# A hybrid decoder layer on one core: the group preparation, group end, substitution and output rows recorded behind the reading of a PSUM bank

## The chip, the cores and the metric

One core of one Trainium2 chip. The metric is the device time of one execution in microseconds (us); times of several executions are given as their median. The engines by the profile's names: PE multiplies matrices (PEld is its weight load), DVE, ACT and POOL work on vectors, SP issues nearly all DMAs. Every engine takes its instructions in the order in which the program recorded them.

## What is computed

One decoder layer over 2048 tokens of 1024 channels, all in float32:

```python
h = rms_norm(x, pre_norm_w)
p = h @ w_in                                  # r k v z + two low ranks | conv | pool | 3 gates
y_a = rwkv7_branch(token_shift(p_rwkv), ...)  # a state of 64 x 64 for each of 8 heads, token by token
y_b = short_conv_branch(p_conv, conv_w)
y_c = pool_branch(p_pool, pool_w, pool_scale)
merged = sum_n sigmoid(p_gate[n]) * (y[n] @ w_branch[n])
x = x + rms_norm(merged @ w_out, post_norm_w)
```

## The kernel before

**Products.** Tokens are handled in two halves of 1024. A *product* (`product`, L180) multiplies a piece of 512 x 128 weights with 512 tokens: 12 matmuls of 128x512, because operands and weights are each split into a high and a low part (`hi`, `lo`; tiles h.., l.., wh, wl) and three of the four combinations are made (L183, L184, L185). ACT makes the high part of the weights (L142), POOL the low one (L144). A `Pair` (L190) makes two tiles of 128 columns for two blocks of 512 tokens in seven products instead of eight: the products T1, T2, T3, T4 work on sums and differences (tiles hT, lT) and are added to others. They share three banks of PSUM, one called `ch` and two called `mm`. So a bank is read in the midst of its use: `act.copy(p1, ch)` after B11 and `act.copy(u2, ch)` after T2; `dve.tensor_tensor(p1, p1, b2)` after B21 (L253), `u2 += bb` after B22 (L257) and `p5 += ch` after T3 (L261). A product that adds to a bank, or begins anew in it, cannot start until that reading is done. T4 of a pair (`last`, through `flush`) is put off until the next pair has made B11 and T1; it adds to the `ch` that L261 reads.

**What runs beside the products.** Each `yield` in a job stands behind a product. There `execute` prepares weights (`supply`), issues stores that are due (`after_product`, which also takes one piece of work from the list `puts`) and advances the *sides* by one step each. I call what is recorded between two products an *interval*. The sides are the RWKV groups (`rwkv_groups`; 16 groups of 128 tokens, groups 0 to 7 in the first half, 8 to 15 in the second), the norm and operands of the second half (`stage_ops`), the mixing of the pooling branch (`mix_pooled`), loads and splits of later operands (`fill`), and sums for the last stage (`out_sums`).

**A group** (`rwkv_group`, L688) has a *main chain*: small matmuls into `rk` banks (16 times 64x128 and so on), their masked copies G on DVE, a store of G to DRAM and a load back as NB, a forward *substitution* of 15 rows on NB and Tt (L760 and L761, two DVE instructions a row, in four portions of 4, 4, 4 and 3 rows), a store of Tt to DRAM (`td`) and a load back as TT, a DVE transpose Td (L777), matmuls with Td (L785), X and TT (L792), a second DVE transpose T1 (L800), matmuls with it (L811), and then the state, chunk by chunk (R, U, state). Beside it run, one step per interval, the *preparation* of the next group (`group_head`: kk, S, ta, f, BK, XA, r) and the *end* of the last group (`group_tail`: d, q, m, y). In `step` (L692) these two are advanced first and then the interval is left, so in the recorded order they stand after the main chain's work and before whatever the job does when it resumes: the reading of the bank. The same holds for the substitution, which stands in the main chain itself.

**The output stage** is eight pairs (`out_pair`) of output rows. For each of the four tiles of a pair, `last` (L1092, L1093: scale by the norm, add x) is put on the list `puts` and taken in a later interval by `after_product`, so before that interval's bank is read.

What sets the order is this, at the head of each interval:

```python
for _ in j.run():          # a job, up to its next yield
    supply(1)
    after_product()        # stores, one of puts
    for side in sides:
        side.advance()     # main chain, then end of the last group, then preparation of the next
```

Of the kernel before, what the change touches and what calls it, by code (L numbers as in the profile page):

```python
# [53 lines left out]
def trunk_kernel(ctx, tc, x, pre_norm_w, post_norm_w, w_in, mu_shift, rwkv_w0, rwkv_w_up,  # L54
# [132 lines left out]
    sums = [pool]  # L187
    tail = [None]

    class Pair:  # L190
# [42 lines left out]
        def run(self):  # L233
# [5 lines left out]
            act.copy(p1[:, 16:], ch)  # L239
            bb = mm_bank()  # L240
# [3 lines left out]
            act.copy(p5[:, 16:], bb)  # L244
            yield from flush()
# [3 lines left out]
            act.copy(u2[:, 16:], ch)  # L249
            b2 = mm_bank()  # L250
            product(b2, take(), ops["B21"], True)
            yield
            dve.tensor_tensor(p1[:, 16:], p1[:, 16:], b2, ALU.add)  # L253
            sink(0, 0, p1[:, 16:], p1)
            product(bb, take(), ops["B22"], False)
            yield
            dve.tensor_tensor(u2[:, 16:], u2[:, 16:], bb, ALU.add)  # L257
            sink(0, 1, u2[:, 16:], u2)
            product(ch, take(), ops["T3"], False)
            yield  # L260
            dve.tensor_tensor(p5[:, 16:], p5[:, 16:], ch, ALU.add)  # L261
            sink(1, 1, p5[:, 16:], p5)

            def last():
                product(ch, take(), ops["T4"], False)
                yield
                sink(1, 0, ch, None)
# [27 lines left out]
    def single(ops, c, sink):  # L295

        def body():
# [6 lines left out]
            act.copy(p1[:, 16:], ba)  # L304
            product(bb, a1, h["T1"], True, False)
            yield
            product(ba, a2, h["B21"], False)
            yield
            first = sink(0, ba)
            product(bb, a2, h["B22"], False)  # L310
            yield
            dve.tensor_tensor(p1[:, 16:], p1[:, 16:], bb, ALU.add)
            second = sink(1, p1[:, 16:])
# [19 lines left out]
    def after_product():  # L333
        for dst, src in stores.pop(0):
            sp.dma_start(dst, src)
        stores.append([])
        if puts:
            puts.pop(0)()
# [192 lines left out]
    def rwkv_single(half, h, c):  # L531
# [8 lines left out]
        def sink(b, val):  # L540
# [6 lines left out]
            def products(upw):  # L547
                (uh, ul) = upw
                for n, bias in enumerate((hw0, ha0)):
                    ns = half_of(n)  # L550
                    for i in range(NCT):
# [7 lines left out]
                        if i == 1:  # L559
                            yield  # L560
                    yield
            return products
# [126 lines left out]
    def rwkv_group(g, head, before, following):  # L689
# [4 lines left out]
        def step(n=1, begin=False):  # L694
            if begin and following is not None:
                after[0] = group_head(following)
            for _ in range(n):
                next(before, None)
                if after[0] is not None:
                    try:  # L700
                        next(after[0])
                    except StopIteration as e:
                        after[0], got[0] = None, e.value
                yield

# [52 lines left out]
        for j in range(15):  # L758
            n = 15 - j
            dve.tensor_tensor(tmp[:, :, :n], bc(NBt[:, j, j + 1:], 1, 8), bc(Tt[:, :, j], 2, n), ALU.mult)  # L760
            dve.tensor_tensor(Tt[:, :, j + 1:], Tt[:, :, j + 1:], tmp[:, :, :n], ALU.add)  # L761
            if j in (3, 7, 11):
# [613 lines left out]
```

## Time and profile before

| | |
|---|---|
| three runs, us | 2309.71, 2313.94, 2318.79 (median 2313.94) |
| the profiled execution, us | 2305.26 |
| its span, first to last instruction, us | 2303.5 |
| PE busy | 2172.0 us, 94% |
| DVE busy | 1398.6 us, 61% |
| POOL busy | 1320.7 us, 57% |
| ACT busy | 896.0 us, 39% |
| mean granted clock of PE | 0.968 |

The span and the views belong to the profiled execution; 1.76 us of its time lie outside the span. It is 8.68 us under the median and 4.45 us under the fastest of the three runs. Roughly, groups 0 to 7 run from 200 to 1010 us, groups 8 to 15 from 1150 to 1900 us, the merge of the branches ends near 2130 us and the output pairs fill the rest. A wait of an engine is idle time in front of an instruction; the profile puts it down to the instruction whose semaphore came last.

### The profile page before, as it was taken

Reading aid. Unit: us, or ns where it says so; the run is one execution under the profiler, and the core shown is the slowest. Engines: PE = TensorE matmul, PEld = TensorE weight load, DVE = VectorE, ACT = ScalarE, POOL = GpSimd, SP = SyncE. Lnnn points to the kernel's source line nnn. Section 1 sums busy time; section 2 is a strip of 40 time slices with the busy share of each in tenths; the row PEclk is TensorE's granted clock in tenths of the full one; section 3 lists DMA queues with packets and bytes.
Section 4 is the critical chain, followed back from the end, with each engine's and each line's share of the span. In section 5 each row is a group of like instructions: output and inputs, shape, how many; then the busy total and the mean of one; then the engine's idle time right before and its main releaser. Section 6 shows DMA issues by size and latency. Waiting matters only on the chain.

```text
span 2303.5 us, 47215 instructions
## 1 busy us (share of the span) xinstructions
PE 2172.0 (94%) x18514; PEld 1752.8 (76%) x18514; DVE 1398.6 (61%) x2214; ACT 896.0 (39%) x1777; POOL 1320.7 (57%) x1105
## 2 busy tenths in 40 slices
PE   5999999999999999989989999899999999999898
PEld 4788777777787877768878787777878788787786
DVE  7413777777848646635476867756475663655754
ACT  5444433442434345444533423244343521313343
POOL 7657565665656555436765655455565445555554
PEclk7989999999999999989999999999999999999999
DMA  3243323243547427343522323355464855898974
GB/s 104 87 142 120 103 62 91 66 141 106 155 131 213 121 89 218 104 159 124 160 83 55 100 54 107 88 166 160 131 186 116 252 147 146 271 315 280 317 223 143
DMA packets 471800, 336.20 MB, mean 146 GB/s; under 512 B 107477, under 2 KB 389274, under 8 KB 471578
## 3 DMA queue, kind: packets, MB, share of 16 engines
q1 hardware_dynamic: 471578, 333.19, 47.8%
q8 instruction: 145, 2.38, 0.4%
q14 instruction: 77, 0.63, 0.1%
HBM read 220.76 MB, written 112.33 MB: 145 GB/s over the span
## 4 chain that ended last, share of the span: by engine, by line
PE 64%; DVE 15%; DMA 5%; issue 5%; ACT 3%; POOL 2%; SPq 1%; DVEq 0%; POOLq 0%; ACTq 0%
PE ch L183 10%; PE ch L185 9%; PE ch L184 9%; PE mm L183 8%; PE mm L184 7%; PE mm L185 7%; DVE Ttmp L760 3%; DVE Tt L761 3%; PE rk L599 2%; PE rk L717 2%; POOL wl L144 1%; PE rk L841 1%; PE rk L833 1%; PE rk L849 1%; DMA ly<-yD 1%
## 5 line engine op out<-in xcount | busy, mean ns | idle before, releaser
L144 POOL TENSOR_TENSOR wl<-ws,wh 128x512 fp32r<-128x512 f32 x492 | 681.9, 1390 | 572.4 <-ACT wh L142 534.8
L142 ACT CAST wh<-ws 128x512 fp32r<-128x512 f32 x492 | 304.1, 619 | 233.7 <-PE mm L184 81.2
L183 PE MATMUL ch<-hT,wh 128*128 128x512 f32 x864 | 357.1, 413 | 29.4 <-DVE p L261 22.3
L185 PE MATMUL ch<-hT,wl 128*128 128x512 f32 x864 | 344.2, 398 | 0.4 <-POOL wl L144 0.4
L184 PE MATMUL ch<-lT,wh 128*128 128x512 f32 x864 | 344.4, 399 | 0.0
L183 PE MATMUL mm<-hB,wh 128*128 128x512 f32 x600 | 241.6, 403 | 2.8 <-ACT p L304 2.8
L184 PE MATMUL mm<-lB,wh 128*128 128x512 f32 x600 | 234.3, 390 | 0.0
L185 PE MATMUL mm<-hB,wl 128*128 128x512 f32 x600 | 234.1, 390 | 0.0
L183 PEld LDWEIGHTS ch<-hT,wh 128*128 128x128 f32 x864 | 167.0, 193 | 73.0 <-issue 22.6
L144 POOL TENSOR_TENSOR wl<-s,wh 128x512 fp32r<-128x512 f32 x64 | 86.7, 1355 | 200.7 <-ACT wh L142 197.0
L185 PEld LDWEIGHTS ch<-hT,wl 128*128 128x128 f32 x864 | 166.6, 193 | 38.0 <-POOL wl L144 1.3
L184 PEld LDWEIGHTS ch<-lT,wh 128*128 128x128 f32 x864 | 167.0, 193 | 32.0
L213 POOL TENSOR_TENSOR ws<-ws,s 128x512 f32<-128x512 f32 x128 | 181.3, 1417 | 1.6 <-DMA ws<-in_w_in 1.6
L1025 POOL TENSOR_TENSOR g<-g 128x512 f32<-128x512 f32 x64 | 86.2, 1353 | 112.5 <-DVE g L1021 97.0
L183 PEld LDWEIGHTS mm<-hB,wh 128*128 128x128 f32 x600 | 112.5, 188 | 29.7 <-ACT p L304 3.6
L183 PE MATMUL mm<-hT,wh 128*128 128x512 f32 x296 | 122.8, 415 | 10.6 <-DVE p L253 7.0
L185 PEld LDWEIGHTS mm<-hB,wl 128*128 128x128 f32 x600 | 112.6, 188 | 24.4
L184 PEld LDWEIGHTS mm<-lB,wh 128*128 128x128 f32 x600 | 112.8, 188 | 21.5
L183 PE MATMUL ch<-hB,wh 128*128 128x512 f32 x288 | 119.7, 416 | 7.0 <-DVE g L1021 3.6
L185 PE MATMUL ch<-hB,wl 128*128 128x512 f32 x288 | 116.5, 404 | 10.4 <-POOL wl L144 10.4
L761 DVE TENSOR_TENSOR Tt<-Tt,Ttmp 128x120 f32<-128x120 f32 (+14 forms) x240 | 117.3, 489 | 8.3
L185 PE MATMUL mm<-hT,wl 128*128 128x512 f32 x296 | 118.7, 401 | 0.0
(281 smaller groups left out, 4625.7 us busy)
## 6 DMA issues: line engine op xcount, KB each, us to landing
ws<-in_w_in SPq DMA_DIRECT2D x260, 256.0 KB
g<-gD SPq DMA_DIRECT2D x96, 256.0 KB
gD<-p SPq DMA_DIRECT2D x48, 256.0 KB
ly<-yD SPq DMA_DIRECT2D x48, 256.0 KB
ws<-in_w_branch SPq DMA_DIRECT2D x48, 256.0 KB
mD<-g SPq DMA_DIRECT2D x32, 256.0 KB
ws<-oD SPq DMA_DIRECT2D x32, 256.0 KB
xr<-in_x SPq DMA_DIRECT2D x32, 256.0 KB
```

The lines of the kernel that those rows point to most:

```text
L142: act.copy(hi, src)
L144: pool.tensor_tensor(lo, src, hi.bitcast(F32), ALU.subtract)
L183: pe.matmul(bank, hi[:, k, :], th[k], start=start and k == 0, stop=False, skip_group_check=True)
L184: pe.matmul(bank, hi[:, k, :], tl[k], start=False, stop=False, skip_group_check=True)
L185: pe.matmul(bank, lo[:, k, :], th[k], start=False, stop=stop and k == HK - 1, skip_group_check=True)
L213: sums[0].tensor_tensor(w[o], w[a], w[b], op)
L599: both(lambda h, hs: pe.matmul(bank[hs, a * 64:a * 64 + 64], src[hs, a], ident[hs, hs], start=True, stop=True))
L717: both(lambda h, hs: pe.matmul(bgs[n][hs, i * P:(i + 1) * P], BK[hs, n, 2 * i + c], XA[hs, 2 * i + c].rearrange("p x t -> p (x t)"), start ...
L760: dve.tensor_tensor(tmp[:, :, :n], bc(NBt[:, j, j + 1:], 1, 8), bc(Tt[:, :, j], 2, n), ALU.mult)
L761: dve.tensor_tensor(Tt[:, :, j + 1:], Tt[:, :, j + 1:], tmp[:, :, :n], ALU.add)
L833: both(lambda h, hs: pe.matmul(r3[hs, i], G[hs, 1, 0, a], vt[hs, a], start=True, stop=False, skip_group_check=True))
L1025: pool.tensor_tensor(acc[b], acc[b], gs[b], ALU.add)
```

## The change

A second kind of yield, `yield READ`, marks the point behind the reading of a bank. A function given to `aside` is run there, and so is one piece of `puts`. The preparation, the end and the four portions of the substitution are given to `aside`; the rest of the main chain and the other sides stay where they were. For groups 8 to 14 the number of intervals between the load of TT and the transpose Td grows from two to three, as groups 0 to 7 have it.

```diff
+    READ = True
+    asides = []
+    def aside(f):
+        asides.append(f)
+    def run_asides():
+        while asides:
+            asides.pop(0)()
...
             product(b2, take(), ops["B21"], True)
             yield
             dve.tensor_tensor(p1[:, 16:], p1[:, 16:], b2, ALU.add)
+            yield READ
             sink(0, 0, p1[:, 16:], p1)
             product(bb, take(), ops["B22"], False)
             yield
             dve.tensor_tensor(u2[:, 16:], u2[:, 16:], bb, ALU.add)
+            yield READ
             sink(0, 1, u2[:, 16:], u2)
             product(ch, take(), ops["T3"], False)
             yield
             dve.tensor_tensor(p5[:, 16:], p5[:, 16:], ch, ALU.add)
+            yield READ
             sink(1, 1, p5[:, 16:], p5)
             def last():
                 product(ch, take(), ops["T4"], False)
                 yield
+                yield READ
                 sink(1, 0, ch, None)
...
         for dst, src in stores.pop(0):
             sp.dma_start(dst, src)
         stores.append([])
-        if puts:
-            puts.pop(0)()
...
             for _ in range(n):
-                next(before, None)
-                if after[0] is not None:
-                    try:
-                        next(after[0])
-                    except StopIteration as e:
-                        after[0], got[0] = None, e.value
+                aside(beside)
                 yield
+        def beside():
+            next(before, None)
+            if after[0] is not None:
+                try:
+                    next(after[0])
+                except StopIteration as e:
+                    after[0], got[0] = None, e.value
...
-        for j in range(15):
-            n = 15 - j
-            dve.tensor_tensor(tmp[:, :, :n], bc(NBt[:, j, j + 1:], 1, 8), bc(Tt[:, :, j], 2, n), ALU.mult)
-            dve.tensor_tensor(Tt[:, :, j + 1:], Tt[:, :, j + 1:], tmp[:, :, :n], ALU.add)
-            if j in (3, 7, 11):
-                yield from step()
-        yield from step(1, True)
+        def substitute(js):
+            for j in js:
+                n = 15 - j
+                dve.tensor_tensor(tmp[:, :, :n], bc(NBt[:, j, j + 1:], 1, 8), bc(Tt[:, :, j], 2, n), ALU.mult)
+                dve.tensor_tensor(Tt[:, :, j + 1:], Tt[:, :, j + 1:], tmp[:, :, :n], ALU.add)
+        for j in range(0, 15, 4):
+            aside(lambda: substitute(range(j, min(j + 4, 15))))
+            yield from step(1, j == 12)
...
-        yield from step(3 if g < 8 else 2)
+        yield from step(3 if g < 15 else 2)
...
-            for _ in j.run():
-                supply(1)
-                after_product()
-                for side in sides:
-                    side.advance()
+            for read in j.run():
+                if read:
+                    run_asides()
+                    if puts:
+                        puts.pop(0)()
+                else:
+                    supply(1)
+                    after_product()
+                    for side in sides:
+                        side.advance()
+            run_asides()
         if not first:
             for _ in flush():
-                after_product()
+                pass
             while puts or stores[0] or stores[1]:
+                if puts:
+                    puts.pop(0)()
                 after_product()
```

The other readings of a bank (the ACT copies of a `Pair`, `single`, the products of the low ranks, `merge_tile`) get a `yield READ` in the same way, and `Side.finish` runs the asides after each step. The first group of each half has its preparation before the chain begins, as steps of its own that are not given to `aside`.

Three places in the recorded order, all on DVE. The first is the substitution of group 4, in a gate pair: `u..` is u2 += bb (L257), `p..<-..ch` is p5 += ch (L261; L277 in the changed file), Ttmp and Tt are the rows of the substitution, d is the end of group 3. Before:

```order
L257 TENSOR_TENSOR u_6851<-u_6851,mm 128x512
L760 TENSOR_TENSOR Ttmp<-NB,Tt 128x8x7
L761 TENSOR_TENSOR Tt<-Tt,Ttmp 128x8x7
L760 TENSOR_TENSOR Ttmp<-NB,Tt 128x8x6
L761 TENSOR_TENSOR Tt<-Tt,Ttmp 128x8x6
L760 TENSOR_TENSOR Ttmp<-NB,Tt 128x8x5
L761 TENSOR_TENSOR Tt<-Tt,Ttmp 128x8x5
L760 TENSOR_TENSOR Ttmp<-NB,Tt 128x8x4
L761 TENSOR_TENSOR Tt<-Tt,Ttmp 128x8x4
L675 TENSOR_TENSOR d<-d,v 128x512
L261 TENSOR_TENSOR p_6785<-p_6785,ch 128x512
```

And with the change:

```order
L272 TENSOR_TENSOR u_6850<-u_6850,mm 128x512
L786 TENSOR_TENSOR Ttmp<-NB,Tt 128x8x11
L787 TENSOR_TENSOR Tt<-Tt,Ttmp 128x8x11
L786 TENSOR_TENSOR Ttmp<-NB,Tt 128x8x10
L787 TENSOR_TENSOR Tt<-Tt,Ttmp 128x8x10
L786 TENSOR_TENSOR Ttmp<-NB,Tt 128x8x9
L787 TENSOR_TENSOR Tt<-Tt,Ttmp 128x8x9
L786 TENSOR_TENSOR Ttmp<-NB,Tt 128x8x8
L787 TENSOR_TENSOR Tt<-Tt,Ttmp 128x8x8
L277 TENSOR_TENSOR p_6780<-p_6780,ch 128x512
L786 TENSOR_TENSOR Ttmp<-NB,Tt 128x8x7
L787 TENSOR_TENSOR Tt<-Tt,Ttmp 128x8x7
```

Each reading has moved ahead of one portion of the substitution (and of the d beside it); the portion before that still stands in front of it.

The second place is group 8, a conv pair, where the transpose Td follows kk of the next preparation. Before:

```order
L261 TENSOR_TENSOR p_12140<-p_12140,ch 128x512
L877 SCALAR_TENSOR_TENSOR silu<-silu,p_12140 128x512
L904 TENSOR_TENSOR u_11963<-u_11963,silu 128x512
L608 TENSOR_TENSOR kk<-k,vec 128x512
L777 STREAM_TRANSPOSE Td<-TT 128x512
L877 SCALAR_TENSOR_TENSOR silu<-silu,ch 128x512
L904 TENSOR_TENSOR p_11842<-p_11842,silu 128x512
L621 SCALAR_TENSOR_TENSOR S<-smask,sw 128x512
```

With the change:

```order
L277 TENSOR_TENSOR p_12140<-p_12140,ch 128x512
L904 SCALAR_TENSOR_TENSOR silu<-silu,p_12140 128x512
L931 TENSOR_TENSOR u_11963<-u_11963,silu 128x512
L630 TENSOR_TENSOR kk<-k,vec 128x512
L904 SCALAR_TENSOR_TENSOR silu<-silu,ch 128x512
L931 TENSOR_TENSOR p_11842<-p_11842,silu 128x512
L804 STREAM_TRANSPOSE Td<-TT 128x512
L643 SCALAR_TENSOR_TENSOR S<-smask,sw 128x512
```

Td now stands behind one more interval, that of the product T4 whose bank silu reads. Every later group of this half begins one interval later than the one before it did, seven in all at the end.

The third place is the second output pair: so, post and xr belong to the output rows (L1092, L1093; L1120, L1121 in the changed file), lm to the sums for later pairs. Before:

```order
L257 TENSOR_TENSOR u_22292<-u_22292,mm 128x512
L1092 SCALAR_TENSOR_TENSOR p_22208<-p_22208,so,post 128x512
L1093 TENSOR_TENSOR xr<-xr,p_22208 128x512
L1058 TENSOR_TENSOR lm<-lm 128x256
L1059 TENSOR_TENSOR lm<-lm 128x256
L1060 TENSOR_TENSOR lm<-lm 128x2x128
L1061 TENSOR_TENSOR lm<-lm 128x2x128
L261 TENSOR_TENSOR p_22234<-p_22234,ch 128x512
```

With the change:

```order
L272 TENSOR_TENSOR u_22290<-u_22290,mm 128x512
L1086 TENSOR_TENSOR lm<-lm 128x256
L1087 TENSOR_TENSOR lm<-lm 128x256
L1088 TENSOR_TENSOR lm<-lm 128x2x128
L1089 TENSOR_TENSOR lm<-lm 128x2x128
L277 TENSOR_TENSOR p_22234<-p_22234,ch 128x512
L1120 SCALAR_TENSOR_TENSOR p_22206<-p_22206,so,post 128x512
L1121 TENSOR_TENSOR xr<-xr,p_22206 128x512
```

The output row's two instructions have moved behind the reading of `ch`.

## Rows read from the trace of the kernel before

**Rows 1.** The page: busy time of PE and DVE, and the chain by engine.
```profile
PE 2172.0 (94%) x18514; PEld 1752.8 (76%) x18514; DVE 1398.6 (61%) x2214; ACT 896.0 (39%) x1777; POOL 1320.7 (57%) x1105
...
PE 64%; DVE 15%; DMA 5%; issue 5%; ACT 3%; POOL 2%; SPq 1%; DVEq 0%; POOLq 0%; ACTq 0%
```
**Rows 2.** Timeline of PE, first matmuls of two products: start, length, instruction, [idle before <-releaser].
```profile
698.37 0.39 PE L183 MATMUL mm<-hT,wh 128*128 128x512 f32 x1
...
703.31 0.47 PE L183 MATMUL ch<-hT,wh 128*128 128x512 f32 x1 [2.06 <-DVE Ttmp L760]
```
**Rows 3.** What PE waited for, 1200 to 1850 us: total, times, longest.
```profile
PE rk L785 <- DVE Td L777: 11.0, 5, 3.6
PE ch L183 <- DVE p L261: 6.3, 2, 6.1
PE mm L183 <- DVE p L253: 3.5, 1, 3.5
PE mm L183 <- DVE p L920: 3.5, 1, 3.5
PE rk L811 <- DVE T L800: 2.2, 2, 1.9
```
**Rows 4.** The same, 300 to 1010 us.
```profile
PE rk L811 <- DVE T L800: 6.9, 3, 5.3
PE rk L390 <- DVE xt L466: 4.5, 2, 3.7
...
PE ch L183 <- DVE Ttmp L760: 2.1, 1, 2.1
...
PE rk L599 <- DVE d L665: 1.2, 1, 1.2
```
**Rows 5.** The same, 2130 to 2304 us.
```profile
PE ch L183 <- DVE p L261: 8.8, 4, 4.5
```
**Rows 6.** Stretches: us, PE, PEld, DVE, ACT, POOL busy; granted clock; DMA share; GB/s.
```profile
1492.30:1499.13 6.83, 5.01 (x12) 3.98 (x13) 5.96 (x10) 2.75 (x6) 3.91 (x4) 0.50 0.98 295
1499.13:1505.96 6.83, 6.83 (x32) 5.65 (x31) 5.23 (x5) 1.61 (x3) 4.72 (x4) 1.00 0.56 164
...
1799.50:1802.91 3.41, 3.41 (x10) 2.64 (x9) 0.41 (x3) 3.00 (x8) 2.86 (x3) 0.50 0.84 282
...
2174.97:2181.79 6.82, 5.96 (x14) 4.73 (x15) 2.07 (x4) 3.65 (x8) 3.75 (x3) 0.50 1.05 334
```
**Rows 7.** Timeline of DVE ahead of a reading, 1490.90 to 1493.97 us.
```profile
1490.90 0.21 DVE L760 TENSOR_TENSOR Ttmp<-NB,Tt 128x56 f32<-128x56 f32 x1
...
1493.29 0.68 DVE L261 TENSOR_TENSOR p<-p,ch 128x512 f32<-128x512 f32 x1
```
**Rows 8.** The same, 1393.37 to 1399.33 us.
```profile
1393.37 0.18 DVE L760 TENSOR_TENSOR Ttmp<-NB,Tt 128x24 f32<-128x24 f32 x1
...
1398.65 0.68 DVE L253 TENSOR_TENSOR p<-p,mm 128x512 f32<-128x512 f32 x1
```
**Rows 9.** Timeline of DVE in the output stage, 2167 to 2176 us.
```profile
2171.03 1.75 DVE L1092 SCALAR_TENSOR_TENSOR p<-p,so,post 128x512 f32<-128x512 f32 x1 [2.04 <-POOL so L498]
...
2173.41 0.42 DVE L1058 TENSOR_TENSOR lm<-lm 128x256 f32<-128x256 f32 x1
...
2175.00 0.68 DVE L261 TENSOR_TENSOR p<-p,ch 128x512 f32<-128x512 f32 x1
```
**Rows 10.** Timeline of DVE after the last product, 2297 to 2301 us.
```profile
2297.60 0.75 DVE L1092 SCALAR_TENSOR_TENSOR o<-ch,so,post 128x512 f32<-128x512 f32 x1 [5.34 <-POOL so L498]
...
2299.00 0.75 DVE L1092 SCALAR_TENSOR_TENSOR p<-p,so,post 128x512 f32<-128x512 f32 x1
```
**Rows 11.** What DVE waited for, whole span: total, times, longest.
```profile
DVE p L253 <- PE mm L185: 52.0, 13, 26.4
...
DVE p L261 <- PE ch L185: 14.3, 12, 3.3
DVE u L257 <- PE mm L185: 11.8, 13, 2.5
```

More of the change, by code (lines that the diff above doesn't have):

```diff
@@ L257, in run @@
             dve.tensor_tensor(u2[:, 16:], u2[:, 16:], bb, ALU.add)
+            yield READ
             sink(0, 1, u2[:, 16:], u2)
@@ L261, in run @@
             dve.tensor_tensor(p5[:, 16:], p5[:, 16:], ch, ALU.add)
+            yield READ
             sink(1, 1, p5[:, 16:], p5)
@@ L266, in last @@
                 yield
+                yield READ
                 sink(1, 0, ch, None)
@@ L304, in body @@
             act.copy(p1[:, 16:], ba)
+            yield READ
             product(bb, a1, h["T1"], True, False)
             yield
+            yield READ
             product(ba, a2, h["B21"], False)
             yield
+            yield READ
             first = sink(0, ba)
@@ L312, in body @@
             dve.tensor_tensor(p1[:, 16:], p1[:, 16:], bb, ALU.add)
+            yield READ
             second = sink(1, p1[:, 16:])
@@ L560, in products @@
                             yield
+                            yield READ
                     yield
+                    yield READ
             return products
@@ L1023, in body @@
                         acc[b] = gs[b]
-                    else:
+                    yield READ
+                    if acc[b] is not gs[b]:
                         pool.tensor_tensor(acc[b], acc[b], gs[b], ALU.add)
@@ L1133, in finish @@
             for _ in self.gen:
-                pass
+                run_asides()
+            run_asides()
             self.done = True
@@ L1336, in execute @@
                 j.begin()
-            for _ in j.run():
-                supply(1)
-                after_product()
-                for side in sides:
-                    side.advance()
+            for read in j.run():
+                if read:
+                    run_asides()
+                    if puts:
[5 more added lines that the diff above has]
+                        side.advance()
+            run_asides()
         if not first:
             for _ in flush():
-                after_product()
+                pass
             while puts or stores[0] or stores[1]:
+                if puts:
+                    puts.pop(0)()
                 after_product()
```

## The prediction

> **What bounds the kernel now.** I began with the page. PE is busy for 94% of the span, and the chain of work that ended last runs through PE for 64% and through DVE for 15% [rows 1]. So PE is the bound, and the change, which moves hardly anything on PE, can win only what PE loses: time in which it stands, and time at the lower clock. Next I read what PE waited for, stage by stage. With groups 8 to 15 the largest item is the transpose Td (11.0 us in five waits); then come readings of a bank, L261 with 6.3 us and L253 with 3.5 and 3.5 (L920 is the instruction right behind L253; the bank is the same) [rows 3]. With groups 0 to 7 the second transpose T leads with 6.9 us, then xt of `stage_ops` with 4.5; the 2.1 us put down to Ttmp are the reading L261 that stands just before it [rows 4]. In the output stage it is L261 alone, 8.8 us [rows 5]. Then I looked at DVE's own timeline ahead of such a wait: it does not idle, it works off portions of the substitution that the program recorded in front of the reading [rows 7, 8], or output rows [rows 9]. Last came the granted clock: behind a long wait PE runs at 0.50 (1.2 instead of 2.4 GHz); 12 matmuls fill 5.01 us there, where 32 fill 6.83 us at 1.00 [rows 6], so that stretch lost 5.01 - 2.6 = 2.4 us besides the wait.
>
> Prices that I use: a product is 12 matmuls, so at full clock 12 x 6.83 / 32 = 2.6 us [rows 6]; a stretch like the one at 1799 us, where 10 matmuls take 3.41 us instead of 10 x 0.213 = 2.1 us, costs 1.3 us [rows 6]. A portion of the substitution and the d beside it took 2.4 us (1490.90 to 1493.29) [rows 7]; the last, shortest portion took 5.3 us (1393.37 to 1398.65) at another place, since single instructions of it then last over a microsecond [rows 8]. A reading takes 0.68 us in both.
>
> **The change, part by part.** The sum is made against the profiled execution (2305.26 us), and what it saves is taken off the median of the runs shown, 2313.94, which is 8.7 us higher.
>
> *One interval more before Td, groups 8 to 14.* Td comes one product later, at least 2.6 us. Of the five waits the longest is 3.6 us, so 1.0 us is left and 10.0 us go [rows 3]. Four of the five were followed by a stretch at 0.50, the one at 1799 us and three like it at 1410, 1512 and 1608; 4 x 1.3 = 5.2 us. I take half, 2.6 us, since another wait may fall into the same place. Together **12.6 us**; the ends are 4 and 15. The seven intervals are no work: the group finishes seven products later, under the merge, and still before `finish`.
>
> *Readings ahead of portions, groups 8 to 15.* Only what stands in the same interval is overtaken; earlier portions stay in front. The wait at 1399 us goes whole, 3.5 us, as the portion in front of it took 5.3 [rows 3, 8], with one stretch of 1.3 us at 0.50. The one at 1494 us loses 2.4 of 6.1 us [rows 3, 7]. The other 3.5 us of L253 I count as nothing: L261 behind it keeps the same work in front, and PE would wait there instead. **7.2 us**; the ends are 0 (every wait moves on to the next reading) and 17 (all 13.3 us of the three rows and the 2.4 + 1.3 us at low clock).
>
> *The same, groups 0 to 7.* The 2.1 us at 703 us go, with 1.3 us of clock [rows 2, 4]; of xt's 4.5 us a portion of 2.4, as xt now stands ahead of it [rows 4, 7]. The d of a group's end (L665), for which PE waited 1.2 us [rows 4], gets a reading of 0.7 us in front of it: minus 0.7. The 6.9 us on T stay; the work ahead of that transpose is the same. **5.1 us**; the ends are minus 4 (each of the 14 portions pushes a wait of the chain by some tenths) and 10.
>
> *Output rows.* At 2175 us L261 overtakes L1092 and L1093: 2.4 us of work (2171.03 to 2173.41) and the 2.04 us for which L1092 itself waited for POOL; that covers all but a tenth of the longest wait, 4.4 of 4.5 us. The four lm in front of the reading (1.6 us) then fill the gap [rows 5, 9]. Two more of the four waits lose two such instructions each, 1.4 us apart [rows 5, 10]: 2.8 us. The stretch at 0.50 behind the first wait holds 14 matmuls in 5.96 busy us instead of 3.0: 3.0 us more [rows 6]. Against it: the last flush takes no `puts` any more, so the row of u is added behind o, 1.4 us at the very end, where nothing covers it [rows 10]. **8.8 us**; the ends are 3 and 11.
>
> *What comes back.* The extra intervals give groups 9 to 15 another phase against the seven products of a pair, that of groups 0 to 7. There T cost 6.9 us, here 2.2 [rows 3, 4]. I take the difference off, **minus 5**; the ends are minus 12 and 0.
>
> The moved work also issues DMAs on SP (loads of the next group, z) and small instructions on POOL and ACT. On SP they change places only with loads of other sides in the same interval, so I cost them at nothing; the cover is the interval itself.
>
> Sum: 12.6 + 7.2 + 5.1 + 8.8 - 5 = 28.7 us, so 2313.9 - 28.7 = 2285; I say **2286 us**, or 2277 for a profiled execution like this one.
>
> The clock holds 8.2 us of that sum (2.6 + 1.3 + 1.3 + 3.0). The Trainium skill, TensorE: Matmul & The Clock Gate, section "Loop structure matters more than you think", has it that DVE's copying of a result out of PSUM doesn't break PE's clock when the next matmuls follow at once; by that these 8.2 us would be nothing and the time 2293. Here the next matmuls did not follow at once, and the trace has 0.50 behind a wait of 6.1 us on such a reading [rows 3, 6]; I keep the clock in.
>
> **The rivals.**
>
> *The wait moves on.* DVE has the same work; a reading that comes early only lets PE arrive earlier at the next wait. For it: three readings follow each other in a pair, and only the last portion is overtaken. Against it: DVE is busy for 61% of the span [rows 1], so a backlog ends soon. Terms two and three are then 0, the clock is not regained: 10.0 + 5.8 - 5 = 10.8 us, 2303.
>
> *All readings come in time.* The rest of the 13.3 us goes (7.4), the chain's waits do not grow (5), and the clock is regained in full (2.6 + 2.4): 28.7 + 17.4 = 46 us, 2268. For it: the 5.3 us portion [rows 8]. Against it: earlier portions still stand in front.
>
> *Slower: the reading blocks the work behind it.* DVE goes by order. It stood 52.0 + 14.3 + 11.8 = 78 us in 38 waits in front of these three readings for PE [rows 11]. Today the portion or preparation is done before such a wait; then it would begin only after it, and the next step of the main chain (Td, T, U) stands behind it. If in each of 14 groups one matmul of the chain came late by one portion, 2.4 us, with 1.3 us of clock, that is 52 us against 28.7: 23 us slower, 2337. It decides the sign from 8 of the 14 groups on (28.7 / 3.7). Against it: the waits of 52.0 us hold one of 26.4, far from a group's work, and with the portions in progress DVE is late, not early [rows 7, 8]. The Trainium skill, PSUM — Partial Sum Buffer, section "Engine vs sequencer instructions", gives the rule behind it: the queues of the vector engines are strictly first in, first out. The trace agrees that they wait so [rows 11].
>
> **How the numbers follow.** The forecast gets 0.60, the wait that moves on 0.20, all readings in time 0.12, the slower case 0.08. A measurement of this kernel can tell 0.5%, 11.6 us, from no change: faster means under 2302.4, slower over 2325.5. Faster: 0.57 of the first, 0.03 of the second, all of the third, 0.72. Same: 0.20. Slower: 0.08. The range reaches from the third case's 2268 to 2310, just beyond the second; that leaves out the slower case and some 0.08 more.
>
> **What would show it.** Td as a wait of PE all but gone between 1200 and 1850 us; L261 under 2 us in the output stage; no stretch at 0.50 near 2175; L253 and L261 together under 7 us with groups 8 to 15; T at 5 us or more there; the tail from the last matmul to the end 1.4 us longer. DVE's busy time stays within 1%. I am wrong if PE's waits for Td, T, X and U grow by more than those for readings fall, if waits for weights (wl) appear, or if the mean granted clock does not rise.

## The result and the profile after

The changed kernel takes 2329.11 us (median of four runs, 2327.75 to 2332.13), the kernel before 2315.59 us (median of four, 2309.71 to 2318.79). The ratio is 1.0067, 95% interval 1.0051 to 1.0083: 13.5 us **slower** by the medians, 15.5 by the ratio. I had forecast 2286 us and faster. The profiled executions are 2327.75 and 2305.26 us long, their spans 2326.0 and 2303.5. So the two traces lie 22.5 us apart, 9 more than the medians; the trace of before was a good one.

The page of the changed kernel (busy time by engine, and the chain that ended last) answers to [rows 1]. The shares of the chain can't be compared: it could be followed back to 998 us here and to 111 us before, so they add up to 57% and 95% of the span:

```profile
PE 2179.2 (94%) x18514; PEld 1753.2 (75%) x18514; DVE 1412.7 (61%) x2214; ACT 896.9 (39%) x1777; POOL 1328.8 (57%) x1105
...
PE 36%; DVE 9%; DMA 5%; issue 3%; POOL 2%; SPq 1%; ACT 1%; DVEq 0%; POOLq 0%; ACTq 0%
```

The work is the same: DVE 1% more, PE 7 us more. PE's idle times of over 0.4 us add up to 113.6 us before and 125.3 now; its stretches at 0.50, each by the half that it lost, to 75.5 and 82.6 us; from the start of the last matmul to the end it was 8.3 us and is 9.7. These are 11.7 + 7.1 + 1.4 = 20.2 of the 22.5 us.

Where they arise shows from products that both kernels run at a point where each has the same matmuls behind it. Such a matmul starts 4.0 us later at 1011 us of the kernel before (end of group 7), 14.9 us later at 1696, 12.2 at 1792, 26.8 at 1945, and the last one 21.1 us later. So more than half of the loss, 14.6 us, came between 1792 and 1945 us, with groups 14 and 15; only the output stage won.

PE's waits with groups 0 to 7, from 300 to 1010 us (us in total, times, longest), against [rows 4]:

```profile
PE rk L838 <- DVE T L827: 9.0, 3, 6.5
PE rk L621 <- DVE d L687: 4.4, 1, 4.4
PE rk L640 <- ACT sq L631: 3.7, 2, 2.4
PE ch L183 <- ACT u L262: 3.2, 2, 3.0
PE ch L183 <- DVE p L277: 3.0, 2, 2.4
PE ch L183 <- DVE Ttmp L786: 2.9, 1, 2.9
```

T (L827, was L800) went from 6.9 to 9.0 us; d, a step of a group's end, from 1.2 to 4.4; sq, a step of the preparation, is new. The readings (L277 was L261; Ttmp stands for the reading beside it) shrank hardly at all: all of them over 0.3 us, added up from 220 to 1010 us, are 14.4 us after 15.1. From 1200 to 1850 us, against [rows 3]:

```profile
PE ch L183 <- ACT u L262: 8.1, 2, 5.2
PE ch L183 <- DVE p L277: 6.8, 2, 4.5
PE rk L812 <- DVE Td L804: 5.6, 2, 4.5
PE ch L183 <- DVE Ttmp L786: 3.5, 1, 3.5
PE rk L640 <- ACT sq L631: 3.4, 1, 3.4
PE rk L838 <- DVE T L827: 2.7, 4, 1.9
PE rk L621 <- DVE d L687: 1.7, 1, 1.7
```

Td halved, 11.0 to 5.6 us, but readings did not shrink: L253, L920 and L261 had 13.3 us, and here the copies on ACT (L262) wait as well. Behind it, from 1850 to 2140 us, group 15 waits under the merge, where the kernel before waited only for gates:

```profile
PE rk L812 <- DVE Td L804: 4.3, 1, 4.3
PE mm L183 <- DVE g L1048: 3.3, 1, 3.3
```

Added up from 220 to 2000 us of the kernel before (waits over 0.3 us, between matmuls that both kernels run at the same point, without 1011 to 1150 us), PE waits for d and sq 13.2 us instead of 1.2, for readings 38.1 instead of 32.6, and for the main chain 28.1 instead of 25.9. So the waits for steps of the preparation (sq) and the end (d) grew most.

In the output stage, 2140 us to the end, the reading did become shorter (8.8 us in [rows 5]), and a wait for a gate stands at its head (3.6 us at 2126 us before, ahead of the window of [rows 5]):

```profile
PE ch L183 <- DVE g L1048: 4.5, 1, 4.5
PE ch L183 <- DVE p L277: 3.0, 2, 2.1
```

And DVE's last instructions show the row of u behind o, which [rows 10] did not have:

```profile
2320.10 0.74 DVE L1120 SCALAR_TENSOR_TENSOR u<-u,so,post 128x512 f32<-128x512 f32 x1
```

### The profile page after: what moved, and what is told of

Its sections match the earlier page's. It is cut to its first block, busy times and chain, and to the rows that moved or that the text cites. A ratio compares the mean times of both kernels' runs of the same rounds, so it can differ in the third digit from the quotient of the medians.

```text
span 2326.0 us, 47213 instructions
## 1 busy us (share of the span) xinstructions
PE 2179.2 (94%) x18514; PEld 1753.2 (75%) x18514; DVE 1412.7 (61%) x2214; ACT 896.9 (39%) x1777; POOL 1328.8 (57%) x1105
## 4 chain that ended last, share of the span: by engine, by line
PE 36%; DVE 9%; DMA 5%; issue 3%; POOL 2%; SPq 1%; ACT 1%; DVEq 0%; POOLq 0%; ACTq 0%
PE ch L183 6%; PE ch L185 5%; PE ch L184 5%; PE mm L183 4%; PE mm L185 4%; PE mm L184 4%; DVE Tt L787 2%; DVE Ttmp L786 2%; PE rk L742 1%; PE rk L621 1%; POOL wl L144 1%; DMA ly<-yD 1%; DMA g<-gD 1%; DVE win L954 1%; DMA mD<-g 1%
## 5 line engine op out<-in xcount | busy, mean ns | idle before, releaser
L144 POOL TENSOR_TENSOR wl<-ws,wh 128x512 fp32r<-128x512 f32 x492 | 691.1, 1408 | 567.1 <-ACT wh L142 530.6
```

Source lines behind the costliest of these rows:

```text
L144: pool.tensor_tensor(lo, src, hi.bitcast(F32), ALU.subtract)
```

## The experiments

Four parts can be made one at a time: output rows, interval, substitution, preparation and end. (`substitute` and `beside` are the functions of the change; where `beside` is called at once, the order is that of before.) Every ratio is against the kernel before, with its 95% interval; 0.1% is 2.3 us, and differences in us follow the ratio unless said otherwise. Those of the medians are up to 4.4 us off them. Line numbers are those of the changed kernel or two higher; in rows_moved some are one higher.

### One part alone

**rows_alone** (the last flush is that of the changed kernel and takes no `puts`)

```diff
-        if puts:
-            puts.pop(0)()
...
+                if read:
+                    if puts:
+                        puts.pop(0)()
```

> The kernel before, with the output rows alone taken behind the reading. Theory A (preparation and end behind the reading make later steps of the group late), B (the added interval gives groups 8 to 15 a bad phase) and C (the substitution behind the reading is ready too late) all leave this part alone: 4 to 7 us faster (ratio 0.997 to 0.998), L261's wait in the output stage 3 us instead of 8.8, the tail 1.4 us longer. If it is not faster, the output part of the forecast was wrong as well.

Measured: 2310.77 us, 0.9984 (0.9972 to 0.9997), 4 us faster. L277 in the output stage waits 4.7 us, and the time from the last matmul to the end is 9.7 us, 1.4 more, as expected.

**interval_alone**

```diff
-        yield from step(3 if g < 8 else 2)
+        yield from step(3 if g < 15 else 2)
```

> The kernel before, with the third interval before Td for groups 8 to 14 alone. A and C: 4 to 12 us faster, PE's waits for Td between 1200 and 1850 us from 11 us to 1 us, and no other wait takes their place. B: 5 to 15 us slower; the Td waits go, but waits at other lines and waits of group 15 under the merge behind 1900 us come for them.

Measured: 2321.1 us, 1.0030 (1.0018 to 1.0041), 7 us slower: theory B. The trace is that of the longest of its twelve executions (2326.93 us). The waits of PE from 1200 to 1815 us, and from 1815 to 2000:

```profile
PE ch L183 <- ACT u L262: 7.9, 2, 6.0
PE ch L183 <- DVE p L277: 4.4, 1, 4.4
PE mm L183 <- DVE p L267: 3.5, 1, 3.5
PE rk L840 <- DVE T L829: 2.3, 4, 1.2
...
PE rk L814 <- DVE Td L806: 1.1, 1, 1.1
```

```profile
PE ch L183 <- DVE p L277: 9.2, 1, 9.2
PE rk L814 <- DVE Td L806: 3.0, 1, 3.0
```

Td fell from 11.0 to 1.1 us, just as forecast; T stayed at 2.3. But 12.2 us appear behind 1815 us. The 9.2 us (from 1819.4) are put down to a reading, yet DVE's own timeline shows what stood in front of it: until 1822.5 splits of operands of the merge (ly) and two other readings, then 3.5 us of idling ahead of group 14's Td, which waited for its load, then Td itself and S of the next preparation:

```profile
1825.90 0.71 DVE L806 STREAM_TRANSPOSE Td<-TT 128x512 f32<-128x512 f32 x1 [3.45 <-DMA TT<-td]
```

SP's timeline has the trip through DRAM, store (L798) and load (L801), between loads for the merge (L379, 256 KB each):

```profile
1814.62 2.36 SPq L798 DMA_DIRECT2D td<-Tt  x4
1817.07 1.82 SPq L379 DMA_DIRECT2D ly<-yD  x4
...
1820.13 2.94 SPq L801 DMA_DIRECT2D TT<-td  x4
```

The substitution ended at 1812.8 us, so Td came 13.1 us behind it; in the kernel before it was 7.1 for group 14 (1789.5 to 1796.6). The DMA queue's share of its 16 engines from 1810 to 1828 us:

```profile
q1 hardware_dynamic: 7873, 4.86, 95.5%
```

It was 53.9% around the trip of before (1785 to 1800 us), with 4 such loads there and 11 here.

**sub_alone** (preparation and end still in front)

```diff
         for j in range(0, 15, 4):
-            substitute(range(j, min(j + 4, 15)))
+            aside(lambda: substitute(range(j, min(j + 4, 15))))
             yield from step(1, j == 12)
```

> The kernel before, with the four portions of the substitution alone behind the reading. A and B: 3 to 8 us faster, the waits on the readings L253 and L261 with the groups from 13 us down to 6 us or less. C: 5 to 10 us slower, Tt is stored later and PE's waits for Td grow from 11 us to 18 us or more, with ones in groups 0 to 7 too.

Measured: 2338.12 us, 1.0117 (1.0098 to 1.0137), 27 us slower (23 by the medians): theory C and more. PE's order is that of the kernel before, so waits can be paired. PE at one product of a pair, first before, then here, where a later product waits as well (it did not before):

```profile
1208.13 0.47 PE L183 MATMUL mm<-hT,wh 128*128 128x512 f32 x1 [3.52 <-DVE p L253]
```

```profile
1220.90 0.47 PE L183 MATMUL mm<-hT,wh 128*128 128x512 f32 x1 [1.60 <-DVE Ttmp L788]
...
1226.24 0.47 PE L183 MATMUL ch<-hT,wh 128*128 128x512 f32 x1 [2.37 <-DVE p L277]
```

3.5 us became 1.6 + 2.4. The wait at 1399 us [rows 8], which I had counted as gone, became 2.3 + 2.6 us. Why nothing was won shows when DVE's busy time is taken over substitutions alone (window, its length, then busy us of PE, PEld, DVE, ACT, POOL); groups 2, 8 and 10 before, then the same here:

```profile
478.40:499.10 20.70, 16.20 (x95) 12.95 (x94) 19.53 (x47) 4.25 (x10) 10.33 (x12) 0.92 0.37 112
...
1186.20:1209.90 23.70, 20.18 (x88) 16.37 (x87) 21.41 (x44) 5.22 (x9) 11.61 (x9) 0.98 0.34 98
...
1379.10:1398.70 19.60, 16.86 (x101) 13.49 (x99) 18.63 (x35) 5.23 (x11) 12.53 (x10) 1.00 0.41 120
```

```profile
479.90:501.10 21.20, 17.33 (x106) 13.58 (x105) 20.06 (x48) 5.08 (x13) 10.23 (x12) 1.00 0.37 114
...
1200.90:1224.90 24.00, 21.37 (x94) 17.07 (x92) 21.78 (x45) 5.21 (x9) 11.60 (x9) 1.00 0.33 97
...
1396.80:1417.00 20.20, 17.93 (x106) 14.40 (x105) 19.24 (x36) 5.32 (x11) 12.64 (x10) 1.00 0.40 118
```

DVE is busy for 90 to 95% of these stretches either way, as in 15 of the 16 groups before (group 7 has 72%). A full queue that is put in another order is still full: in both pairs, what one reading gained the next one lost. And the chain lost more: Td cost PE 18.4 us in 7 waits from 1150 to 1950 us, 11.0 in 5 before. Added up from 220 to 2000 us as above, waits for the chain went from 25.9 to 36.4 us, and those for readings did not fall, but went from 32.6 to 37.3.

**side_alone**

```diff
             for _ in range(n):
-                beside()
+                aside(beside)
                 yield
```

> The kernel before, with the preparation and the end of the groups alone behind the reading. A: 10 to 25 us slower, with waits of PE for sq and for d (the matmuls with blockones and ident) of 3 us or more each, which the kernel before has hardly at all, and longer ones for T and U. B and C: within 4 us of the kernel before.

Measured: 2318.73 us, 1.0016 (1.0003 to 1.0029), 4 us slower, between the theories. sq (1.9 us) and d (4.4 us) came as theory A said, but its sum was far too large. Two more runs split this part.

**head_alone** (`head_step` is the second half of `beside`)

```diff
                 next(before, None)
-                head_step()
+                aside(head_step)
                 yield
```

> The kernel before, with the preparation alone behind the reading. Preparation and end together were 4 us slower. If it is the preparation (its sq and f come late for the matmuls with blockones, which then hold PE 1 to 2 us), this is 3 to 5 us slower (1.0015 to 1.002); if it is the end (d late for the matmuls with ident, 4.4 us near 592 us), this is within 2 us of the kernel before.

Measured: 2314.85 us, 0.9998 (0.9988 to 1.0009): nothing.

**tail_alone**

```diff
-                next(before, None)
+                aside(lambda: next(before, None))
                 head_step()
                 yield
```

> The kernel before, with the end of the groups alone behind the reading. If it is the end that costs, as preparation alone left the time at 0.9998 and both together gave 1.0016, this is 2 to 6 us slower (1.001 to 1.0025), with PE's waits for d at 3 us or more near 592 us. If only both together cost, it is within 2 us of the kernel before.

Measured: 2321.55 us, 1.0031 (1.0017 to 1.0045), 7 us slower. The end is the costly half; PE before the matmuls with ident, where the kernel before waited 1.2 us, is the clearest item:

```profile
595.49 1.58 PE L623 MATMUL rk<-ident,d 64*64 64x64 f32 x32 [4.43 <-DVE d L689]
```

How 1.2 became 4.4 us shows on DVE some 17 us earlier, at a reading that waits for PE, first before, then here:

```profile
577.15 0.69 DVE L253 TENSOR_TENSOR p<-p,mm 128x512 f32<-128x512 f32 x1 [0.98 <-PE mm L185]
```

```profile
578.00 0.69 DVE L267 TENSOR_TENSOR p<-p,mm 128x512 f32<-128x512 f32 x1 [2.17 <-PE mm L185]
```

Before, DVE made an earlier step of the end (gst) while PE finished the product; here gst comes behind the reading. POOL's part of gst then starts at 582.98 instead of 577.35 us, POOL's cnt for the pooling branch stands behind it, and DVE waits 2.7 instead of 1.7 us for cnt. All in all DVE is 1.9 us later, measured against PE, and d falls behind xt and the next reading, another 1.4 us: 3.3 in all. The other 4 of the 7 us are not traced to a place.

### Parts taken out of the whole change

**no_sub** (against the changed kernel)

```diff
-            aside(lambda: substitute(range(j, min(j + 4, 15))))
+            substitute(range(j, min(j + 4, 15)))
```

> The changed kernel with the substitution alone put back in front of the reading; preparation, end, output rows and the added interval stay as changed. If the substitution costs in the whole change what it cost alone (23 to 27 us), this is 8 to 11 us faster than the kernel before (ratio 0.995 to 0.9965). If the parts simply add, -4 for the rows, +7 for the interval and +4 for preparation and end, it is 7 us slower (1.003). The second means that the added interval takes back most of the substitution's loss in the whole change.

Measured: 2321.61 us, 1.0028 (1.0015 to 1.0042). The three other parts simply add. So in the whole change the substitution costs 0.4%, 9 us (7 by the medians), and not the 27 us that it costs alone. No run takes preparation and end out of the whole change, where the waits for their steps grew most.

**no_interval** (against the changed kernel)

```diff
-        yield from step(3 if g < 15 else 2)
+        yield from step(3 if g < 8 else 2)
```

> The changed kernel without the added interval (two before Td for groups 8 to 14, as before). If the parts add, the interval's +7 us goes and this is 8 to 10 us slower than the kernel before (1.004). If the interval makes good what the later substitution costs Td, it is 20 to 30 us slower (1.009 to 1.013), with PE's waits for Td between 1200 and 1850 us at 12 us or more.

Measured: 2330.0 us, 1.0076 (1.0059 to 1.0093), between the two expectations. Beside the late substitution the added interval is no loss any more: with it the ratio is 1.0067. Why substitution, preparation and end together are cheaper than the substitution alone is open; in sub_alone the portion also falls behind the preparation and end of its own interval, which might be it.

**sub_last_front** (against sub_alone)

```diff
-            aside(lambda: substitute(range(j, min(j + 4, 15))))
+            if j < 12:
+                aside(lambda: substitute(range(j, min(j + 4, 15))))
+            else:
+                substitute(range(j, 15))
```

> The kernel before, with the first three portions of the substitution behind the reading and the fourth in front as before, so that Tt is stored as early as the portions allow. If the loss of the substitution alone (23 to 27 us) is the chain's, a later store of Tt and later Td, most of it goes: within 5 us of the kernel before, Td waits back at 11 us. If it is the readings', each portion standing in front of the next reading instead, it stays: 15 us slower or more (1.0065), with waits on readings after L253 as with all four portions behind.

Measured: 2330.3 us, 1.0079 (1.0060 to 1.0098), 18 us slower. Two thirds of the loss stay though Tt is not held back by a reading of its own. Not as I said, though, through readings alone: L277 has 7.3 us from 1150 to 1950 us, and Td still 14.6. From 220 to 2000 us PE waits 36.5 us for the chain, as in sub_alone, and 35.8 for readings.

**rows_flush** (rows_alone, and in the end)

```diff
-            for _ in flush():
-                pass
+            for read in flush():
+                if not read:
+                    after_product()
+                    if puts:
+                        puts.pop(0)()
```

> The output rows alone behind the reading, and the last flush takes one of them as the kernel before does. 1 to 2 us faster than with the rows alone, so 5 to 6 us faster than the kernel before (0.9975); the time from the last matmul to the end 1.4 us shorter than with the rows alone. If the tail's row was covered anyway, the same as the rows alone, 0.9984.

Measured: 2305.83 us, 0.9965 (0.9951 to 0.9978), 8 us faster than the kernel before: **the best of all versions run that do the whole work**. From the start of the last matmul to the end it is 8.3 us again, 1.4 less than in rows_alone; the rest of the difference between the two lies within their intervals. L277 in its output stage:

```profile
PE ch L183 <- DVE p L277: 3.2, 2, 2.4
```

### What the interval and the order could have given

**interval_idle** (before, at the end of `rwkv_group`)

```diff
+        if 8 <= g < 15:
+            yield from step()
         for _ in before:
             yield
```

> The kernel before, with one interval more in each of groups 8 to 14, as in the interval alone, but at the end of the group where nothing waits for it; Td keeps its two. If the loss of the interval alone (7 us) comes from moving the groups seven products against the rest of the program, this is slower by 7 us plus what Td's waits keep, 7 to 15 us (1.003 to 1.0065), with the waits of 6 us near 1519 and of 9 us near 1829 and one of group 15 behind 1900 us again. If it comes from the place of the interval ahead of Td, this is within 3 us of the kernel before.

Measured: 2318.71 us, 1.0014 (1.0004 to 1.0025), 3 us slower, on the edge of the second expectation. The waits speak for the first: 6.1 us for u, 9.0 us at 1817 us, now put down to Td itself, and 3.3 us of group 15 at 1917 us all came. Td's earlier waits went too (one of 1.0 us is left), since the groups stand elsewhere against the products. So the shift alone is enough to remove Td's earlier waits and to bring the late ones. Of the 7 us it brought 3, and the intervals of the two runs overlap, so whether the place of the interval costs the rest is not shown.

**rows_moved** (rows_flush; groups 8 to 15 get three intervals before Td and lose one earlier)

```diff
         turned(0)
-        yield from step()
+        if g < 8:
+            yield from step()
...
-        yield from step(3 if g < 8 else 2)
+        yield from step(3)
```

> The rows with the last flush, and in groups 8 to 15 three intervals before Td, paid for by the interval between the two turned copies of BK, which is left out: no group moves against the products. If the shift into the loads of the merge was the loss, the gain that the forecast saw now comes: PE's waits for the chain between 1150 and 1815 us fall from 14 us to 5 us or less, no wait of 9 us near 1820 us, and the time is 5 to 12 us under that of the rows with the last flush (0.9965), so 0.991 to 0.9945. If the interval ahead of Td is bad by itself, it is 3 us or more slower than that kernel (0.998 or over).

Measured: 2310.69 us, 0.9982 (0.9968 to 0.9996), 4 us slower than rows_flush: the gain did not come. Yet the first theory's waits did: none near 1820 us, and 0.3 us for Td in all. From 1150 to 2000 us:

```profile
PE ch L183 <- DVE p L277: 8.9, 3, 5.1
PE rk L621 <- DVE d L687: 6.9, 3, 3.8
...
PE rk L640 <- ACT sq L631: 2.1, 2, 1.2
```

In place of Td PE waits 9.0 us for d and sq, which the kernel before did not do there at all: the portions, one interval earlier, now stand in front of d.

**rows_moved_late** (against rows_moved, in `group_tail`)

```diff
         yield
         yield
+        if g >= 8:
+            yield
         bt = rk_bank()
         quarters(bt, ct(d))
```

> rows_moved with one interval more between d and its matmuls with ident in the ends of groups 8 to 15. The 9 us of waits of PE for d and sq fall to 3 us or less; with the chain at 5 us and no wait near 1820 us the time is 5 to 9 us under rows_moved (0.9945 to 0.996). If the waits only go on to the next reader of DVE's queue, it stays at 0.998, with the readings longer by what d loses.

Measured: 2313.92 us, 0.9996 (0.9983 to 1.0009). The waits went on: d and sq 7.4 us, and readings grew by 5 us.

**rows_spread5** (against rows_flush)

```diff
-        for j in range(0, 15, 4):
-            substitute(range(j, min(j + 4, 15)))
-            yield from step(1, j == 12)
+        for j in range(0, 15, 3):
+            substitute(range(j, min(j + 3, 15)))
+            yield from step(1, j + 3 >= 15)
```

> The rows with the last flush, and the substitution in front of the reading in five portions of three rows (one interval more) instead of four. If DVE is simply full in those intervals (19 us of work in four of them), whatever the order, smaller portions shorten the waits on readings with the groups: 5 us or more faster than the rows with the last flush alone (under 0.994). If the shift of the groups decides, it gives back 7 us or more as the interval alone did: 0.9995 or over.

Measured: 2324.15 us, 1.0041 (1.0026 to 1.0056). The shift decided: PE waited 13.9 us for L277 at 1839 us, with group 14's Td in front of it waiting 10.5 us for its load.

**rows_spread8a** (against rows_flush; `rows` takes the place of the 3 above)

```diff
+        rows = 2 if g < 8 else 4
```

> The same with eight portions of two rows in groups 0 to 7 only; groups 8 to 15 as before. A full DVE: the waits on readings near 299, 494 and 703 us (6 to 8 us with the lower clock) go, 3 to 6 us faster than the rows with the last flush alone (0.994 to 0.995). The shift of the groups: slower than that kernel, since 32 intervals move groups 1 to 7 into other pairs and group 7 into the norms of the second half.

Measured: 2331.02 us, 1.0071 (1.0057 to 1.0084). The 32 added intervals bring waits of 5 us each for xt, T, R and d.

**sub_quarter** (before, with 11 of 15 rows of each substitution left out)

```diff
-            substitute(range(j, min(j + 4, 15)))
+            substitute(range(j, j + 1))
```

> The kernel before with 4 of the 15 rows of the substitution in each group, the first of each portion; 11 rows are left out and the output with them, so its time only shows what they cost. If portions in front of readings cost PE what the forecast held (13 us of readings, 5 to 8 us of clock, and Td's waits), it is 20 to 35 us faster (0.985 to 0.991). If DVE's work there hardly costs PE anything, under 10 us, no order of it could have given 12 us.

Measured: 2262.55 us, 0.9772 (0.9753 to 0.9792), **53 us** less, more than I expected. From 1150 to 2000 us PE waits for readings hardly any more:

```profile
PE rk L814 <- DVE Td L806: 6.8, 3, 5.8
PE mm L183 <- DVE g L1050: 3.3, 1, 3.3
PE ch L183 <- DVE p L277: 2.6, 3, 2.2
```

From 220 to 2000 us waits for readings fell from 32.6 to 9.0 us, for the chain from 25.9 to 20.2. So PE pays for the work itself: leaving most of it out gave 53 us, while the best order gave 8, none of it from the substitution, and the worst cost 27. The 53 us hold more than the queue, though: with 11 rows fewer Tt is also stored and loaded earlier, and no run separates the two.

All of PE's waits of over 0.3 us, added up by me (us; "chain" is Td, X, T, U and the like, "side" is d and sq; the border at 1815 us lies up to 25 us earlier in the program of a slower kernel, which puts group 14's Td, 2.2 us, behind it in sub_alone):

| kernel | 1150 to 1815: readings | chain | side | 1815 to 2000: all |
|---|---|---|---|---|
| before | 17.0 | 14.8 | 0.0 | 0.5 |
| after | 18.7 | 8.9 | 1.7 | 13.2 |
| interval_alone | 19.6 | 4.2 | 0.0 | 12.2 |
| interval_idle | 19.7 | 1.8 | 0.0 | 13.4 |
| sub_alone | 19.4 | 14.0 | 0.0 | 6.2 |
| rows_moved | 17.0 | 4.3 | 9.0 | 1.0 |
| rows_moved_late | 22.0 | 6.7 | 7.4 | 1.5 |
| sub_quarter | 2.2 | 7.7 | 0.0 | 3.6 |

## Why the prediction was wrong

**One interval more (minus 12.6 us forecast, plus 7 measured alone).** The term had the size of what it looked at: Td's waits fell by 9.9 us where I had said 10.0. That the third interval did it is not shown by that run, since the shift alone does the same (interval_idle); without the shift three intervals leave 0.3 us (rows_moved), which speaks for the mechanism. The step that failed is "The seven intervals are no work: the group finishes seven products later, under the merge". A group that is moved takes its two trips through DRAM with it. Those of group 14 fell into the loads and splits of the merge's operands, and the late Td and the splits held up the reading behind them on DVE: 12.2 us behind 1815 us. interval_idle and rows_spread5 move the groups and get that wait; rows_moved doesn't move them and hasn't got it. That the interval wins without the shift is not shown: rows_moved turned the gain into waits for d. And within the whole change the interval cost nothing that can be told (1.0067 with it, 1.0076 without).

**Readings ahead of portions (minus 7.2 and minus 5.1 forecast, plus 27 alone, plus 9 within the change).** This is the largest miss. The step that failed is in the rival of the wait that moves on: "DVE is busy for 61% of the span, so a backlog ends soon". 61% is the mean; in the substitutions it is 90 to 95%. I had the rows for it (a portion of 5.3 us in an interval whose product takes 2.6) and read only the span. So I took the length of the overtaken portion off the wait, and it came back at the next reading (3.5 us became 1.6 + 2.4). The term's lower ends, 0 and minus 4, also left out the rest: I had a wait of the chain grow by some tenths, and in sub_alone the chain's waits grew by 10.5 us. Why the same move costs 9 us instead of 27 beside the other parts stays open.

**Preparation and end (minus 0.7 forecast for d, plus 4 measured, 7 for the end alone).** Two steps failed. The first is "gets a reading of 0.7 us in front of it": d's wait grew from 1.2 to 4.4 us, since an earlier step of the end had fallen behind a reading that itself waits for PE, and since d stands behind xt as well. The second is the sentence on the small instructions on POOL, "so I cost them at nothing": it looks at SP alone, and a late gst on POOL made DVE wait 1.1 us longer. The preparation by itself cost nothing, as I had it (0.9998), but in the whole change its sq alone has waits of 7.1 us, and with d they are 12.0 us more than before. What that part costs there no run shows.

**Output rows (minus 8.8 forecast, minus 4 measured, minus 8 with the flush mended).** Right in kind, too large in size: L261's 8.8 us fell to 3.0 to 4.7. The term that missed is "all but a tenth of the longest wait, 4.4 of 4.5 us": 2.1 to 3.8 us of that wait are left. The four lm, which were to fill the gap, waited there for their own load, 0.7 (after), 1.1 (rows_flush) and 1.4 us (rows_alone). The 1.4 us at the very end are there to the tenth. Nothing of a group's chain stands behind the rows there.

**What comes back (plus 5 us for T).** In groups 8 to 15 T stayed at 2.3 to 2.7 us. The new phase was paid at other places.

**The clock (8.2 us forecast).** 75.5 us were lost at 0.50 before and 82.6 after; but rows_alone, with the same groups, shows 83.3. What a single trace shows there moves by 8 us between executions, so no term of a few us can be read from it. The mean granted clock, whose rise was to be a sign of being right, went from 0.968 to 0.965.

The rival "the reading blocks the work behind it" had 0.08 and 2337 us; 2329 is near it, partly by luck: its 52 us of late chain did not come, nor did the 28.7 us of gain set against them. Its place (portion and chain late) is what sub_alone shows, mixed with the wait that moves on. My two rivals were one: in these full stretches the same swap did both. The Trainium skill, PSUM — Partial Sum Buffer, section "Engine vs sequencer instructions", has these queues as strictly first in, first out; the pairs of waits in sub_alone (3.5 to 1.6 + 2.4 us) agree.

## What to carry to other kernels

Before putting one piece of work behind another on an engine, take its busy share over just the stretch in which the piece runs, not over the span. Here it was 90 to 95% where the substitution runs, and no order of it that was tried won anything, while less work did. In the output stage (59% from 2140 to 2290 us before) the new order did pay, if the last piece isn't left without cover. And an added interval moves everything behind it, transfers first; ask where the last of them lands.

## What the runs showed of the hardware

I had not expected how much POOL lengthens the portions. In [rows 8] an instruction of the substitution that takes 0.2 us elsewhere takes 1.2 to 1.3 us from 1393.58 us on; the first and the last such instruction:

```profile
1393.58 1.28 DVE L761 TENSOR_TENSOR Tt<-Tt,Ttmp 128x24 f32<-128x24 f32 x1
...
1397.35 1.18 DVE L760 TENSOR_TENSOR Ttmp<-NB,Tt 128x8 f32<-128x8 f32 x1
```

POOL's timeline of the kernel before has a gap just ahead of that, and then no pause:

```profile
1387.27 1.29 POOL L144 TENSOR_TENSOR wl<-ws,wh 128x512 fp32r<-128x512 f32 x1
1393.53 1.28 POOL L677 TENSOR_TENSOR d<-d,z 128x512 f32<-128x512 f32 x1 [4.96 <-DVE d L675]
1394.77 1.29 POOL L144 TENSOR_TENSOR wl<-ws,wh 128x512 fp32r<-128x512 f32 x1
...
1397.24 1.26 POOL L144 TENSOR_TENSOR wl<-ws,wh 128x512 fp32r<-128x512 f32 x1
```

Each small instruction of DVE lasts about as long as one of POOL. The Trainium skill, SBUF — State Buffer, section "SBUF: two separate sides", says that a DVE instruction with two inputs in SBUF and a POOL instruction that reads SBUF share a pair of ports, and that whoever starts first holds it for the whole instruction; the trace agrees. No run here took POOL's work away, but group 7 comes near it. The same 30 instructions of the substitution took 7.0 us of DVE's time there, and 18.2 in group 14. The stretches of the two (window, its length, then busy us of PE, PEld, DVE, ACT, POOL):

```profile
987.40:1003.90 16.50, 13.29 (x73) 9.29 (x72) 11.84 (x42) 6.99 (x13) 0.50 (x2) 0.80 0.11 34
1769.30:1789.50 20.20, 20.20 (x117) 16.56 (x117) 19.27 (x34) 8.51 (x17) 14.36 (x12) 1.00 0.54 160
```

So part of what fills DVE's queue is POOL's work, which no run moved. POOL thus makes the length of a portion a matter of what POOL does just then: group 4's fourth portion took 1.2 us before and 6.4 in sub_alone.
